# Neighbourhood attention taken in pairs of steps, with scores and transposes in one ring of four PSUM banks

## The chip, the cores and the metric

One core of one Trainium2 chip. The metric is the device time of one execution in microseconds; the kernel before is given by the median of three runs. Times of parts come from one profiled execution of it.

## The reference

One layer of an encoder, applied to two token groups, `x_prompt` (1024 tokens, 16 rows of 64) and `x_sample` (512 tokens, 8 rows): RMSNorm, two-dimensional neighbourhood attention with residual, RMSNorm, SwiGLU with residual, a final RMSNorm. Only the attention matters here. Width 1024, 16 heads of 64; a query at grid row r sees 8 rows of keys, and in them the 16 columns around its own, which are taken as bands of 32 columns for 16 query columns each:

```python
s = jnp.einsum('bjqhd,bkjchd->bhjqkc', qr, kr) * scale       # j: 4 column blocks, c: 32 key columns
s = jnp.where(valid_j, s + bias, -jnp.inf)
p = softmax(s over (k, c))                                    # 8 rows x 32 columns
o = jnp.einsum('bhjqkc,bkjchd->bjqhd', p, vr)
...
x = x + o @ w_o
x = x + swiglu(rms_norm(x, norm_ffn), w_gate, w_up, w_down)
```

All data is float32.

## The kernel before, in words

**Precision.** Every float32 operand of a large matmul is split into a high and a low half (`split`, lines 138 and 139 without scale: ScalarE (ACT) casts, VectorE (DVE) subtracts), and a product is made of three passes (`PASS`: high-high, high-low, low-high).

**Stages.** Norm of all tokens and V (0 to 180 us of the profile); attention (180 to 735 us); second norm and its operands; a feed-forward part with seven products in place of eight blocks (lines 708 to 819 and 837 to 937), which takes the rest. PSUM has eight banks of 128 x 512 float32. One pool holds four rings of two banks each: tag G for projections, S for scores, T for transposes, V for products. A ring's tile waits until the tile that had its bank before has been read.

**A step of attention.** The heads go in 8 pairs (hp), whose two heads lie on partitions 0 to 63 and 64 to 127. The prompt has per head pair two groups g of 512 queries, the sample one; per group there are four column blocks j. A step is one (hp, g, j): 64 steps in the prompt, 32 in the sample. `step` emits it in this order:

- `scores`, first half (line 394): three passes for two heads, six matmuls of 64 rows each into two S banks.
- `flip` of the step before (lines 420 to 424): each head's probabilities are transposed in 128 x 128 blocks (three in the prompt, two in the sample) into a T bank; ACT copies the high half to tile `pT` (423), DVE subtracts the low half (424).
- `scores`, second half: for each head DVE adds the bias and takes the maximum (402), ACT takes the exponential and the sum (405), DVE the reciprocal (407); head 0 is scaled by DVE (409), head 1 by ACT (411).
- Fillers: portions of six matmuls (lines 332 and 586) of other work, namely the next head pair's Q and K projections and, in the sample, the output projection. Four portions a projection; the last one also evacuates it (lines 342 to 350). Twelve matmuls a step in the prompt.
- `weighted` for the step before (431): products of V with pT into two V banks. Two steps (j = 0, 1 or 2, 3) share them, and after the second one `collect` adds the parts (441 ACT, 442 and 444 DVE) into `oT`, and GpSimd's queue stores it.

After a step come `fill_bias`, which allots and loads bias tiles ahead (lines 198 to 216; three ahead, ring of four; column blocks 1 and 2 share one), and `chores.do`: one weight or V block, loaded earlier by SyncE's queue (SP), is split by ACT and DVE (138 to 142), and the next is loaded. Two loads are under way at a time. V blocks are four DMAs each (line 378).

**Order.** The framework's planner takes the instructions in the program's order as priority and puts them into each engine's queue by its own estimates of when they are ready; each engine then runs its queue in order. So the queues follow the text above in the main, with exceptions where the planner found something not ready.

Of the kernel before, what the change touches and what calls it, by code (L numbers as in the profile page):

```python
# [55 lines left out]
def body(tc, xp, xs, g_mix, g_ffn, g_fin, w_qkv, rpb, w_o, w_g, w_u, w_d, yp, ys):  # L56
# [9 lines left out]
    with es:  # L66
# [39 lines left out]

        def psum(tag, name, bufs=None):
            return ps.tile([P, 512], F32, tag=tag, name=name, bufs=bufs)

# [14 lines left out]
        def transpose_split(xn, hh, hl, col):  # L124
            for b in range(2):
                pt = psum("T", "pt")
# [68 lines left out]
        q_cm, qpool = pool("qpool", bufs=2)  # L195
        b_cm, bpool = pool("bpool", bufs=4)

# [32 lines left out]
        def fill_bias():  # L230
            while len(ahead) < 3:
                n = next(bias_it, None)
# [182 lines left out]
        def flip(ss, n):  # L415
            out = []
            for s in ss:
                pt = psum("T", "ptt")
                for c in range(n):
                    nc.tensor.transpose(pt[:, c * P:(c + 1) * P], s[:, c * P:(c + 1) * P], ident)  # L420
                pT = ap.tile([P, 3, 2, P], F32R, tag="pT", name="pT", bufs=3)
                pv = pt[:, :n * P].rearrange("p (c q) -> p c q", q=P)
# [23 lines left out]

        def steps(hp, g, q, k, v, n, store):
            oT = ap.tile([P, 512], F32, tag="o", name="oT", bufs=2)
            ov = oT.rearrange("p (r j i) -> p j r i", r=8, j=NJ)
            b = None  # L450
            for jj in range(2):
                pos = []
                for u in range(2):
                    j = jj * 2 + u
                    if j != 2:
                        b = next_bias()
                    yield dict(
                        s=lambda b=b, j=j: scores(q, k, 4 * (g == 1), 4 * n, j, lambda h: b[:, h, :n * P]),
                        n=n, pos=pos, g=u, j=j, v=v,
                        dst=(lambda h, jj=jj: ov[h * HD:(h + 1) * HD, jj * 2:jj * 2 + 2]) if u else None,  # L460
                        done=(lambda: nc.gpsimd.dma_start(out=o_d[hp, :, g * 512:(g + 1) * 512], in_=oT))
                        if j == 3 else None)
                    fill_bias()

# [10 lines left out]

        def step(st, fillers, n):
            sc = st["s"]() if st else None
            if sc:
                next(sc)
            pT = None  # L480
            if prev:
                p, pss = prev.pop()
                pT = flip(pss, p["n"])
            ss = next(sc) if sc else None
            run(fillers, n)
            if pT:
# [50 lines left out]
        for hp in range(HP):  # L537
# [6 lines left out]
            if last:  # L544
# [14 lines left out]
        step(None, [], 0)  # L559
        k_cm.__exit__(None, None, None)  # L560

# [44 lines left out]
        for hp in range(HP):  # L606
# [13 lines left out]
        step(None, ofill, 2)  # L620
        a_cm.__exit__(None, None, None)
# [36 lines left out]
        def norm2(t):  # L658
# [5 lines left out]
            for b in range(2):  # L664
                pt = psum("T", "pt")
                for kk in range(4):
# [290 lines left out]
```

## Time and profile before

| what | us |
|---|---|
| median of 3 runs (lowest, highest) | 1846.19 (1841.29, 1848.37) |
| profiled execution | 1845.18 |
| its span | 1843.4 |
| PE busy in the span | 1754.1 |
| DVE, ACT, GpSimd busy | 1192.9, 863.7, 448.4 |
| attention, prompt (180 to 518.2) | 338.2 |
| attention, sample (518.2 to 735) | 216.8 |

The span is the profiled time from the first to the last instruction; 1.8 us of the execution lie outside it. PE is TensorE's matmuls, PEld its weight loads, which run beside them; SPq and POOLq are queues that issue DMAs. In a row of the timeline stand start, length, engine, line, operation, output tile <- input tiles, shape and count, and in brackets how long the engine had been idle before it and what ended that. Lengths of matmuls include their way through the array, so the next one starts before the last has ended; I reckon PE's time from start to start. In a row of groups stand busy time, mean ns of one, and idle time before.

### The profile page before, as it was taken

How to read it: one execution, taken by the hardware profiler on the slowest of the kernel's cores; microseconds unless marked ns; L12 is line 12 of the kernel's file. 1: busy time of each engine (PE TensorE's matmuls, PEld its weight loads, DVE VectorE, ACT ScalarE, POOL GpSimd, SP SyncE). 2: the span in 40 equal slices, each digit the busy share in tenths (PEclk: the TensorE clock that was granted, in tenths of full speed). 3: DMA queues.
4: the chain of work that ended last, by engine and by line, in shares of the span. 5: the costliest groups of instructions: out<-in, count | busy, mean ns of one | idle time of the engine just before them, and what ended most of it. 6: DMA issues, size and time to landing. Idle time of an engine off the chain costs nothing.

```text
span 1843.4 us, 25648 instructions
## 1 busy us (share of the span) xinstructions
PE 1754.1 (95%) x9178; PEld 1522.5 (83%) x9178; DVE 1192.9 (65%) x2191; ACT 863.7 (47%) x1706; POOL 448.4 (24%) x495
## 2 busy tenths in 40 slices
PE   8999999999999999979999999999999969999898
PEld 6877777777767777868999999899999958887676
DVE  4401877777896566768777777867777444545654
ACT  4411776766785554544443444444443333333322
POOL 1211000000130000112243342424243323526420
PEclk9999999999999999988999999999999979999999
DMA  7755334333464443676343434544333277635732
GB/s 245 221 183 160 111 105 113 108 101 103 126 208 146 133 149 100 221 247 185 108 121 118 133 110 151 164 129 125 108 120 107 68 272 245 225 130 191 232 129 100
DMA packets 222048, 278.80 MB, mean 151 GB/s; under 512 B 25600, under 2 KB 171776, under 8 KB 221920
## 3 DMA queue, kind: packets, MB, share of 16 engines
q1 hardware_dynamic: 201824, 210.69, 37.3%
q0 software_dynamic: 18368, 60.18, 9.5%
q10 hardware_dynamic: 1728, 6.29, 1.1%
q8 instruction: 72, 1.18, 0.3%
q14 instruction: 56, 0.46, 0.1%
HBM read 213.20 MB, written 76.43 MB: 157 GB/s over the span
## 4 chain that ended last, share of the span: by engine, by line
PE 68%; DVE 10%; DMA 9%; ACT 5%; issue 3%; SPq 2%; POOL 2%; DVEq 0%; ACTq 0%; POOLq 0%
PE pa L754 20%; PE pd L910 12%; PE pd L754 10%; PE pgv L278 7%; PE pg L332 6%; PE pb L754 5%; DMA vr<-v_d 5%; PE pgo L586 3%; DMA dr<-ffn_w_down 2%; PE pss L394 2%; PE ptt L420 2%; DVE pT L424 2%; SPq L378 2%; PE po L431 2%; ACT s L405 1%
## 5 line engine op out<-in xcount | busy, mean ns | idle before, releaser
L910 PE MATMUL pd<-wd,go 128*128 128x512 f32 x1386 | 323.0, 395 | 30.5 <-ACT go L138 20.4
L910 PEld LDWEIGHTS pd<-wd,go 128*128 128x128 f32 x1386 | 263.0, 191 | 90.4 <-ACT go L138 21.6
L754 PE MATMUL pa<-h,ws 128*128 128x384 f32 x1056 | 201.8, 339 | 2.9 <-ACT c L777 2.1
L754 PE MATMUL pa<-h,wa 128*128 128x384 f32 x1056 | 195.1, 338 | 7.0 <-ACT wa L138 4.5
L754 PE MATMUL pd<-h,ws 128*128 128x384 f32 x1056 | 198.3, 335 | 1.2 <-ACT h L138 0.6
L332 PE MATMUL pg<-hTp,whl 128*128 128x512 f32 x768 | 193.7, 399 | 0.0
L754 PEld LDWEIGHTS pa<-h,wa 128*128 128x128 f32 x1056 | 185.8, 190 | 8.9 <-ACT wa L138 5.2
L139 DVE TENSOR_TENSOR ws<-wt,ws 128x1024 fp32r<-128x1024 f32 x88 | 108.6, 1235 | 127.1 <-ACT ws L138 126.7
L754 PEld LDWEIGHTS pa<-h,ws 128*128 128x128 f32 x1056 | 185.1, 189 | 6.7 <-ACT c L777 4.3
L754 PEld LDWEIGHTS pd<-h,ws 128*128 128x128 f32 x1056 | 184.5, 188 | 1.8 <-ACT h L138 1.0
L332 PEld LDWEIGHTS pg<-hTp,whl 128*128 128x128 f32 x768 | 139.9, 188 | 27.5 <-issue 0.4
L805 POOL DMA_DIRECT2D gop_d<-c x66 | 50.5, 765 | 387.4 <-DVE c L796 380.3
L405 ACT ACTIVATE s<-s,mx 128x384 f32<-128x384 f32 (+1 forms) x192 | 110.7, 580 | 67.3 <-DVE mx L402 67.1
L586 PE MATMUL pgo<-wo,oh 128*128 128x512 f32 x576 | 139.3, 392 | 0.2 <-DVE oh L139 0.2
L139 DVE TENSOR_TENSOR wa<-wr,wa 128x512 fp32r<-128x512 f32 x132 | 117.8, 897 | 18.4 <-ACT wa L138 17.8
L138 ACT CAST ws<-wt 128x1024 fp32r<-128x1024 f32 x88 | 92.6, 1053 | 68.6 <-PE pd L754 65.4
L586 PEld LDWEIGHTS pgo<-wo,oh 128*128 128x128 f32 x576 | 105.6, 188 | 20.7 <-DVE oh L139 0.6
L138 ACT CAST go<-gr 128x1408 fp32r<-128x1408 f32 x42 | 57.7, 1374 | 131.2 <-PE pd L910 114.0
L138 ACT CAST wa<-wr 128x512 fp32r<-128x512 f32 x132 | 81.4, 621 | 62.8 <-PE pb L754 40.0
L754 PE MATMUL pb<-h,wa 128*128 128x384 f32 x528 | 102.0, 340 | 3.4 <-DVE c L774 3.4
L332 PE MATMUL pg<-hTs,whl 128*128 128x512 f32 x384 | 102.6, 404 | 0.8 <-DVE q L343 0.8
L424 DVE TENSOR_TENSOR pT<-ptt,pT 128x384 fp32r<-128x384 f32 (+1 forms) x192 | 90.0, 507 | 17.3 <-ACT pT L423 16.5
(138 smaller groups left out, 2859.6 us busy)
## 6 DMA issues: line engine op xcount, KB each, us to landing
gr<-gop_d SPq DMA_DIRECT2D x42, 704.0 KB
dr<-ffn_w_down SPq DMA_DIRECT2D x99, 256.0 KB
wr<-ffn_w_gate SPq DMA_DIRECT2D x44, 512.0 KB
wr<-ffn_w_up SPq DMA_DIRECT2D x44, 512.0 KB
wr<-na_w_qkv SPq DMA_DIRECT2D x38, 512.0 KB
gop_d<-gs POOLq DMA_DIRECT2D x88, 192.0 KB, 4.4
gop_d<-c POOLq DMA_DIRECT2D x66, 192.0 KB, 2.8
vr<-v_d SPq DMA_DIRECT2D x192, 64.0 KB
```

What stands on the lines that cost most here:

```text
L138: nc.scalar.copy(hi, raw)
L139: nc.vector.tensor_tensor(lo, raw, f32(hi), ALU.subtract)
L278: nc.tensor.matmul(pg, hh[a][:, k, c:c + P], wv[k // 2][b][:, k % 2], start=(k == 0 and i == 0), stop=(k == KB - 1 and i == 2))
L332: nc.tensor.matmul(pg, w[:, a, k, :], h[b][:, k, c:c + 512], start=(k == 0 and i == 0), stop=(k == KB - 1 and i == 2))
L378: nc.sync.dma_start(out=raw[:, j * P:(j + 1) * P], in_=src[:, BS[j]:BS[j] + 32, :])
L394: nc.tensor.matmul(pt[:, :n], q[h * HD:(h + 1) * HD, a, j].rearrange("p r i -> p (r i)"), kv[:, krow:krow + nrow, BS[j]:BS[j] + 32], start ...
L405: nc.scalar.activation(s[:, :n], s[:, :n], AF.Exp, bias=mx, scale=-1.0, accum_out=sm)
L424: nc.vector.tensor_tensor(pT[:, :n, 1], pv, f32(pT[:, :n, 0]), ALU.subtract)
L586: nc.tensor.matmul(pg, ohs[k // 4][:, a, k % 4], wo[:, b, k, n * 512:(n + 1) * 512], start=(k == 0 and i == 0), stop=(k == KB - 1 and i == 2))
L754: nc.tensor.matmul(bank[:, :HT], a(y, k), b[:, z, k], start=start and k == 0 and i == 0, stop=k == KB // 2 - 1 and i == 2, skip_group_chec ...
L805: nc.gpsimd.dma_start(out=gop_d[i, 3 * c:3 * c + 3, :, p].rearrange("j q t -> q j t"), in_=a.rearrange("q (j t) -> q j t", j=3))
L910: nc.tensor.matmul(pd, go[:, y, i], wds[i][:, z], start=(i == 0 and m == 0), stop=(i == NP - 1 and m == 2))
```

## The change

Two steps, column blocks 0 and 1 or 2 and 3, become one unit. Its twelve score matmuls of both blocks are emitted in one run into four banks of tag S. Then come the softmax of four heads, filler portions (`fill(0)`, two of them in the prompt), the products of the pair before with `collect`, and the two flips of this pair, each followed by one filler portion. The products are so one pair behind their scores, and the flips are in the pair itself. Tag T is gone: transposes take banks of tag S, which has four. Bias tiles are two ahead in a ring of three, `pT` has four buffers in place of three, and the chores of two steps come together after a pair. In the last head pair of the prompt a pair gets three filler portions (one per `fill`), where two steps had two. Transposes of the norms (lines 126 and 665) and one in four of the last products (906) use tag S in place of T.

```diff
         def psum(tag, name, bufs=None):
-            return ps.tile([P, 512], F32, tag=tag, name=name, bufs=bufs)
+            return ps.tile([P, 512], F32, tag=tag, name=name, bufs=4 if tag == "S" else 2)
...
-        b_cm, bpool = pool("bpool", bufs=4)
+        b_cm, bpool = pool("bpool", bufs=3)
...
         def fill_bias():
-            while len(ahead) < 3:
+            while len(ahead) < 2:
...
         def flip(ss, n):
...
-                pt = psum("T", "ptt")
+                pt = psum("S", "ptt")
...
-                pT = ap.tile([P, 3, 2, P], F32R, tag="pT", name="pT", bufs=3)
+                pT = ap.tile([P, 3, 2, P], F32R, tag="pT", name="pT", bufs=4)
...
         def steps(hp, g, q, k, v, n, store):
...
             for jj in range(2):
-                pos = []
-                for u in range(2):
-                    j = jj * 2 + u
+                sc = []
+                for j in (jj * 2, jj * 2 + 1):
                     if j != 2:
                         b = next_bias()
-                    yield dict(
-                        s=lambda b=b, j=j: scores(q, k, 4 * (g == 1), 4 * n, j, lambda h: b[:, h, :n * P]),
...
-                    fill_bias()
+                    sc.append(lambda b=b, j=j: scores(q, k, 4 * (g == 1), 4 * n, j, lambda h: b[:, h, :n * P]))
+                yield dict(s=sc, n=n, jj=jj, v=v, dst=...)
+                fill_bias()
...
-        def step(st, fillers, n):
-            sc = st["s"]() if st else None
-            if sc:
-                next(sc)
-            pT = None
-            if prev:
-                p, pss = prev.pop()
-                pT = flip(pss, p["n"])
-            ss = next(sc) if sc else None
-            run(fillers, n)
-            if pT:
-                if not p["g"]:
-                    p["pos"].extend((psum("V", "po"), psum("V", "po")))
-                weighted(pT, [x() for x in p["v"]], p["j"], p["n"], p["pos"], p["g"])
-                if p["dst"]:
-                    collect(p["pos"], p["dst"])
+        def step(st, fill):
+            sc = [x() for x in st["s"]] if st else []
+            for x in sc:
+                next(x)
+            ss = [next(x) for x in sc]
+            fill(0)
+            if prev:
+                p, pT = prev.pop()
+                pos = [psum("V", "po") for _ in range(2)]
+                for u in range(2):
+                    weighted(pT[u], [x() for x in p["v"]], p["jj"] * 2 + u, p["n"], pos, u)
+                collect(pos, p["dst"])
                 if p["done"]:
                     p["done"]()
+            pT = []
+            for u, x in enumerate(ss):
+                pT.append(flip(x, st["n"]))
+                fill(1 + u)
             if st:
-                prev.append((st, ss))
+                prev.append((st, pT))
...
+            def fill(part):
+                run(fillers, 1 if part or last else 2)
...
                 for st in steps(hp, g, (q0, q1)[g], k, vs[g:g + 3], 3, None):
-                    step(st, fillers, 1 if last else 2)
-                    if i in (0, 1, 2, 5, 6, 7) or last:
-                        chores.do()
-                    i += 1
+                    step(st, fill)
+                    for _ in range(2):
+                        if i in (0, 1, 2, 5, 6, 7) or last:
+                            chores.do()
+                        i += 1
...
+            def fill(part):
+                run(fillers, 1 if part else 2)
+                run(ofill, 1 if part else 2)
+
             for i, st in enumerate(steps(hp, 2, *qk, vs, 2, None)):
-                step(st, fillers, 2)
-                run(ofill, 2)
-                for _ in range((i + 1) * n // 4 - i * n // 4):
+                step(st, fill)
+                for _ in range((i + 1) * n // 2 - i * n // 2):
                     chores.do()
...
-                pd = psum("GSVT"[bank % 4], "pd")
+                pd = psum("GSVS"[bank % 4], "pd")
```

More of the change, by code (lines that the diff above doesn't have):

```diff
@@ L105, in in_order, with psum @@
                         mybir.DependencyClass.NoSync, mybir.DependencyReason.DATA), reason="in_order")
-        def psum(tag, name, bufs=None):
-            return ps.tile([P, 512], F32, tag=tag, name=name, bufs=bufs)
+        def psum(tag, name):
+            return ps.tile([P, 512], F32, tag=tag, name=name, bufs=4 if tag == "S" else 2)
         def bcast(ap):
@@ L125, in transpose_split @@
             for b in range(2):
-                pt = psum("T", "pt")
+                pt = psum("S", "pt")
                 for kk in range(4):
@@ L451, in steps @@
             for jj in range(2):
-                pos = []
-                for u in range(2):
-                    j = jj * 2 + u
+                sc = []
+                for j in (jj * 2, jj * 2 + 1):
                     if j != 2:
                         b = next_bias()
-                    yield dict(
-                        s=lambda b=b, j=j: scores(q, k, 4 * (g == 1), 4 * n, j, lambda h: b[:, h, :n * P]),
[L459 to L462, printed above, removed]
-                    fill_bias()
+                    sc.append(lambda b=b, j=j: scores(q, k, 4 * (g == 1), 4 * n, j, lambda h: b[:, h, :n * P]))
+                yield dict(s=sc, n=n, jj=jj, v=v, dst=lambda h, jj=jj: ov[h * HD:(h + 1) * HD, jj * 2:jj * 2 + 2],
+                           done=(lambda: nc.gpsimd.dma_start(out=o_d[hp, :, g * 512:(g + 1) * 512], in_=oT))
+                           if jj else None)
+                fill_bias()
         def run(fillers, n):
@@ L552, in body @@
                 for st in steps(hp, g, (q0, q1)[g], k, vs[g:g + 3], 3, None):
-                    step(st, fillers, 1 if last else 2)
-                    if i in (0, 1, 2, 5, 6, 7) or last:
-                        chores.do()
-                    i += 1
+                    step(st, fill)
[3 more added lines that the diff above has]
+                        i += 1
             drain(fillers)
             qk = nqk
-        step(None, [], 0)
+        step(None, lambda part: None)
         k_cm.__exit__(None, None, None)
@@ L619, in body @@
             qk = nqk
-        step(None, ofill, 2)
+        step(None, lambda part: run(ofill, 1))
         a_cm.__exit__(None, None, None)
@@ L664, in norm2 @@
             for b in range(2):
-                pt = psum("T", "pt")
+                pt = psum("S", "pt")
                 for kk in range(4):
```

## The prediction

> **What bounds the kernel now.** I read the page first, then a table by stage, then PE's timeline step by step.
>
> ```profile
> span 1843.4 us, 25648 instructions
> PE 1754.1 (95%) x9178; PEld 1522.5 (83%) x9178; DVE 1192.9 (65%) x2191; ACT 863.7 (47%) x1706; POOL 448.4 (24%) x495
> ```
>
> PE is busy 95% of the span, so a gain must come out of PE's idle time or make its work shorter. Only the attention changes. The table by stage (length, busy time of PE, PEld, DVE, ACT and POOL with instruction counts, granted clock, DMA share, GB/s), cut where the head pairs and the two request groups begin, has the prompt's first seven head pairs in rows 1 to 3, its last one in row 4, the sample in rows 5 to 7; the eighth row, of another cut, is the stage behind:
>
> ```profile
> 180.00:264.20 84.20, 81.10 (x468) 63.64 (x468) 66.23 (x191) 58.48 (x144) 5.87 (x15) 1.00 0.36 103
> 264.20:307.60 43.40, 42.00 (x242) 32.91 (x242) 34.51 (x99) 30.46 (x75) 3.09 (x8) 1.00 0.37 106
> 307.60:483.70 176.10, 167.92 (x962) 131.63 (x962) 138.14 (x393) 121.64 (x297) 12.38 (x32) 1.00 0.39 111
> 483.70:518.20 34.50, 33.47 (x189) 24.23 (x189) 30.67 (x90) 30.43 (x73) 6.57 (x6) 1.00 0.45 140
> 518.20:568.90 50.70, 46.50 (x256) 34.97 (x256) 45.66 (x123) 40.12 (x98) 17.15 (x8) 1.00 0.64 195
> 568.90:712.70 143.80, 138.69 (x723) 108.38 (x722) 85.34 (x256) 73.25 (x189) 7.60 (x14) 1.00 0.44 136
> 712.70:735.00 22.30, 22.30 (x130) 17.61 (x130) 16.48 (x54) 13.19 (x39) 2.17 (x4) 1.00 0.20 72
> ...
> 700.00:850.00 150.00, 136.01 (x664) 113.71 (x663) 100.47 (x198) 73.71 (x152) 17.55 (x30) 0.92 0.64 207
> ```
>
> Attention takes 555 us, and PE is bound there too. Rows 1 to 3 are 303.7 us for 7 x 4 pairs of steps, 10.85 a pair; DVE works (66.23 + 34.51 + 138.14) / 28 = 8.53 us of it, ACT 210.58 / 28 = 7.52. PE's timeline of one undisturbed step (start, length, instruction), with the score run cut open by narrower windows (its 2nd and 3rd couple of matmuls start at 302.61 and 302.79):
>
> ```profile
> 301.53 0.87 PE L431 MATMUL po<-pT,v 128*128 128x256 f32 x6
> 302.12 0.28 PE L431 MATMUL po<-pT,v 128*128 128x256 f32 x1
> 302.33 0.81 PE L394 MATMUL pss<-kp,q 64*128 64x384 f32 x6
> 302.61 0.52 PE L394 MATMUL pss<-kp,q 64*128 64x384 f32 x4
> 302.79 0.34 PE L394 MATMUL pss<-kp,q 64*128 64x384 f32 x2
> 303.06 0.87 PE L420 MATMUL ptt<-ident,s 128*128 128x128 f32 x6
> 303.69 3.01 PE L332 MATMUL pg<-hTp,whl 128*128 128x512 f32 x12
> 306.54 0.87 PE L431 MATMUL po<-pT,v 128*128 128x256 f32 x6
> 307.58 0.44 PE L394 MATMUL pss<-kp,q 64*128 64x384 f32 x2 [0.17 <-ACT kp L349]
> ```
>
> Start to start: scores 0.73, transposes 0.63, twelve projection matmuls 2.85, products 0.80: 5.01 a step, 10.02 a pair. So 10.85 - 10.02 = 0.83 a pair, 23.1 us over 28 pairs, is stall. The last row shows one kind: at a new head pair the scores wait for the evacuation of K. The others, ACT, DVE and PE together:
>
> ```profile
> 278.30 0.62 ACT L138 CAST v<-vr 128x512 fp32r<-128x512 f32 x1 [1.91 <-DMA vr<-v_d]
> 279.33 1.02 DVE L424 TENSOR_TENSOR pT<-ptt,pT 128x384 fp32r<-128x384 f32 x2 [2.06 <-ACT pT L423]
> 279.94 1.09 PE L431 MATMUL po<-pT,v 128*128 128x256 f32 x6 [0.41 <-DVE pT L424]
> ...
> 287.49 0.52 PE L420 MATMUL ptt<-ident,s 128*128 128x128 f32 x3 [0.21 <-DVE ri L407]
> 288.34 0.55 PE L420 MATMUL ptt<-ident,s 128*128 128x128 f32 x3 [0.33 <-ACT s L411]
> ```
>
> ACT stands in its queue before a V split whose load has not landed; the copies of pT behind it are late, DVE's subtractions behind those, and the products wait. Eight microseconds on, transposes wait for the softmax. In the sample, three starts of score runs:
>
> ```profile
> 599.44 0.63 PE L394 MATMUL pss<-ks,q 64*128 64x256 f32 x6
> 607.38 0.63 PE L394 MATMUL pss<-ks,q 64*128 64x256 f32 x6
> 614.50 0.38 PE L394 MATMUL pss<-ks,q 64*128 64x256 f32 x1
> ```
>
> A clean step is 614.50 - 607.38 = 7.12, the one before it took 7.94. The stretch of 143.8 us has 19 steps, from its 114 score matmuls, six a step:
>
> ```profile
> L394 PE MATMUL pss<-ks,q 64*128 64x256 f32 x114 | 11.9, 315 | 0.0
> ```
>
> So 143.8 - 19 x 7.12 = 8.5 us are stalls there.
>
> **The change, part by part.** *One score run instead of two.* A score run costs more than its couples' pace of 0.18 (302.61 to 302.79): entry is 0.21 after the last product where products follow each other at (302.12 - 301.53) / 5 = 0.12, the first couple takes 0.28, and from the last couple to the transposes 0.27. That is 0.09 + 0.10 + 0.09 = 0.28 us a run, in a change between 64-row and 128-row matmuls. One run less a pair saves 0.28; 32 prompt and 16 sample pairs give 13.4 us. The bounds: nothing, if the planner cuts the run up again, and these 13.4, since the three surpluses are all that the rows show.
>
> *Products one pair behind.* Now pT is used 2.85 us after its transposes, one projection block. Then the second flip is followed by 6 projection matmuls (1.4), 12 scores (1.27) and 12 projection matmuls (2.85): 5.5 us. The ACT wait of 1.91 then fits inside. I count waits of the products at nothing; the cover is the twelve matmuls of fill(0), and where it lacks (the last pair of the prompt, whose 8 filler portions are spent 3, 3, 2, 0) up to 2 us show once.
>
> *Softmax of four heads, then two flips.* From the groups of one head pair (busy, mean ns):
>
> ```profile
> L405 ACT ACTIVATE s<-s,mx 128x384 f32<-128x384 f32 x16 | 9.8, 614 | 6.3 <-DVE mx L402 6.2
> L402 DVE CUSTOM_DVE_ANT_0 s<-pss,bp 128x384 f32<-128x384 f32 x16 | 8.4, 549 | 0.1
> L424 DVE TENSOR_TENSOR pT<-ptt,pT 128x384 fp32r<-128x384 f32 x16 | 8.2, 551 | 2.1 <-ACT pT L423 2.1
> L423 ACT CAST pT<-ptt 128x384 fp32r<-128x384 f32 x16 | 6.9, 479 | 1.4 <-PE ptt L420 1.4
> L411 ACT ACTIVATE s<-s,ri 128x384 f32<-128x384 f32 x9 | 5.5, 616 | 1.6 <-DVE ri L407 1.6
> L442 DVE TENSOR_TENSOR tmp<-tmp,po 64x256 f32<-64x256 f32 x8 | 3.4, 419 | 3.6 <-ACT tmp L441 3.5
> L139 DVE TENSOR_TENSOR v<-vr,v 128x512 fp32r<-128x512 f32 x4 | 2.8, 689 | 0.0
> L350 DVE TENSOR_TENSOR kp<-pg,kp 128x512 fp32r<-128x512 f32 x3 | 2.1, 692 | 0.9 <-ACT kp L349 0.9
> L139 DVE TENSOR_TENSOR whl<-wr,whl 128x1024 fp32r<-128x1024 f32 x1 | 1.2, 1224 | 0.8 <-ACT whl L138 0.8
> ```
>
> Count from the start of the score run. PE reaches the first flip at 1.27 + 2.85 + 12 x 0.12 = 5.55, the second after six transposes and six projection matmuls, 0.63 + 1.43 later, at 7.6. From the first reduction, the first two heads need about 0.55 + two exponentials 1.23 + reciprocal and scaling, about 0.8, with hand-overs 2.8 us; the other two 2 x 0.61 + 0.62 more, 4.7. So DVE may begin as late as 2.8 (5.55 - 2.8; 7.6 - 4.7 = 2.9). The scores are there at 0.8; ahead of them in DVE's queue stand the last subtractions of pT (to about 0.2), a Q or K subtraction 0.69 and the weight chores, now done back to back behind the pair: a V split 0.69, or V and a Q or K weight 1.91. That is 1.6 in pairs with one chore, 2.8 in pairs with two: no slack left in those. I take 0.5 us of stall in the 14 two-chore pairs and 0.15 in the other 14: 9 us, with ends at 0 and 14 x 1.2 (a whole weight subtraction shown).
>
> *Four banks in one ring.* Scores now wait for the banks of the flips before them. The second flip at 7.6 has its last subtraction 0.3 (three transposes) + 0.48 + 2 x 0.55 later, at 9.5, with hand-overs 9.9; the scores that take these banks start at 9.74 + 0.5. Slack about 0.5 us, so nothing in the plain case. DVE gets there in time only because the four additions of the products (4 x 0.42) lie ahead of the flips; they start at 5.55 and are done by 7.3.
>
> *The boundary of head pairs.* The last portion of K's projection now stands directly before the next head pair's scores; the products that hid it (0.80) are gone. Today's 0.17 becomes 0.17 + 0.80 = 0.97, and the second pass reads the low half, 0.69 of DVE later, part of it under the first couples: 1.3, seven times, 9 us. Ends: 0.17 (PE is given other matmuls meanwhile) and 1.7.
>
> *Biases, SP, POOL.* Three bias buffers with two ahead: the tile for the second step is loaded once the step before has been reduced, about 8 us ahead of its use, against two issues of about 0.6 us on SP; POOL's fills move with it. V loads are issued in twos at a pair's end and used at the next one's; their number is the same. I cost these at nothing: the cover is a whole pair, 9.74 us, and if a load lands late it costs what today's V splits show, 1.91 on ACT.
>
> **The sum.** Prompt, seven head pairs: stalls 23.1 now, 9 + 9 = 18 after, gain 5. Sample: of 8.5 us of stall I take half away, 4 us, since the waits of products go but ACT still meets late loads. Row 4 and row 5: the dense chores stay; the bare last pair costs about 1.5. In all 13.4 + 5 + 4 - 1.5 = 21 us. The profiled execution took 1845.2 us (span 1843.4 and 1.8 around it), 1.0 below the median of 1846.2. 1845.2 - 21 = 1824.2, on the median's scale 1825.
>
> **The rivals.** *The ring closes a loop (slower).* Place: the release of a flip's bank. V splits still stand in ACT's queue; if one waits just ahead of the second flip's copies, subtraction, bank, next scores and the whole of PE shift by it, where today scores and transposes own two banks each. It decides from a stall of 10.85 - 9.74 = 1.1 us a pair. Every prompt pair has a V split, and the waits of 180 to 520 us show
>
> ```profile
> ACT v L138 <- DMA vr<-v_d: 20.5, 12, 2.8
> ```
>
> that is 1.7 us each. At 1.7 in each of 28 pairs, and nothing gained in the sample: 28 x 0.6 = 17 more, 1863. For it: DVE has 8.53 of 9.74 us to do; against it: slack 0.5 at that point, and loads issued a pair ahead.
>
> *The run is cut up.* The planner already split a run (307.58 is a run of two scores, then transposes). If it does so in each pair, the 13.4 us are not gained: 1838.
>
> *The ring never waits.* Stalls are left at the boundaries alone, seven times 1.0, and the sample's go: 13.4 + 16 + 8.5 = 38 gained, 1808.
>
> *The clock.* All seven rows of attention show a clock of 1.00, though PE idled 555.0 - 532.0 = 23 us there in short pieces; the stage behind shows 0.92. If waits on banks took attention to 0.92, 532 us of PE work would grow by 46: 1871. The Trainium skill, "TensorE: Matmul & The Clock Gate", section "A second HAM failure mode: psum-queue depth-cycling", says that a kernel cycling through PSUM banks can pause PE often enough between groups to swing its clock. By that rule the change, with its one ring, would end at the last time named; by this trace, which has such pauses at full clock, it does not.
>
> **How the numbers follow.** Forecast 0.50, ring without waits 0.14, run cut up 0.18, closed loop 0.15, clock 0.03. 0.5% is 9 us, about what a measurement of this kernel can tell from no change, so the borders are 1837 and 1855. Faster: the forecast but for its upper tail, 0.46, 0.14, and the lower end of the cut-up case, 0.05: 0.65. Slower: the loop, the clock, less the loop's mild end: 0.16. The rest 0.19. The range reaches from just below the ring without waits, 1806, to 1850, between the cut-up run and the loop; 0.07 lie below, 0.13 above. The forecast's own range is 1812 to 1838.
>
> **What would show it.** Right: the score run comes as twelve matmuls, starts of head pairs lie 40 to 42 us apart (43.4 now), products wait for nothing, couples inside the run keep 0.18. Wrong: PE rows of scores with idle time ended by DVE's pT subtraction (the loop), score runs of two, four or six (cut up), transposes ended by ACT's scaling for over 0.5 us in most pairs. The stages outside attention should keep their lengths within 3 us; a gain there would have another cause. What would most easily make the forecast wrong is the order in which ACT and DVE get chores and copies, which no row of before shows.

## The result, and the profile after

| | median us | runs |
|---|---|---|
| before | 1846.19 | 7, 1841.29 to 1852.67 |
| changed | 1838.88 | 7, 1832.59 to 1841.12 |

The ratio is 0.9949, interval 0.9926 to 0.9972: 0.5% faster, by the medians 7.3 us, where 21 us were forecast. The time lies in the range; the sign was right, the size a third. Page of the changed kernel, its span and its engines:

```profile
span 1830.8 us, 25624 instructions
PE 1745.4 (95%) x9178; PEld 1529.2 (84%) x9178; DVE 1190.4 (65%) x2191; ACT 858.2 (47%) x1706; POOL 449.2 (25%) x495
```

This execution (1832.59 us) was the shortest of the seven. The same kernel once more, for a second profile, had a median of 1834.2 us (4 runs, ratio 0.9929, interval 0.9907 to 0.9951) and a profiled span of 1837.1. Tables by stage, cut at the second head pair, the last one, the sample, the last product of attention and the end of the feed-forward (length, busy PE, PEld, DVE, ACT, POOL, granted clock, DMA share, GB/s), first the changed kernel:

```profile
220.90:480.30 259.40, 249.18 (x1441) 199.03 (x1440) 205.09 (x589) 180.91 (x445) 19.51 (x48) 0.99 0.40 111
480.30:517.90 37.60, 35.46 (x204) 27.78 (x203) 34.35 (x96) 31.59 (x76) 7.43 (x8) 1.00 0.45 134
517.90:728.20 210.30, 200.49 (x1076) 160.75 (x1076) 142.93 (x422) 119.30 (x317) 26.40 (x26) 0.98 0.47 145
728.20:1470.90 742.70, 726.29 (x4076) 709.00 (x4075) 536.59 (x723) 321.47 (x535) 238.37 (x259) 0.99 0.45 139
1470.90:1830.80 359.90, 322.82 (x1389) 263.14 (x1387) 189.87 (x204) 120.03 (x173) 123.38 (x89) 0.95 0.57 195
```

and the kernel before at the same points:

```profile
220.20:483.70 263.50, 251.88 (x1442) 197.46 (x1442) 207.13 (x589) 182.51 (x445) 18.57 (x48) 1.00 0.38 110
483.70:518.20 34.50, 33.47 (x189) 24.23 (x189) 30.67 (x90) 30.43 (x73) 6.57 (x6) 1.00 0.45 140
518.20:733.90 215.70, 206.38 (x1099) 160.03 (x1100) 146.91 (x430) 125.82 (x323) 26.91 (x26) 1.00 0.46 144
733.90:1481.30 747.40, 728.97 (x4071) 708.90 (x4069) 537.08 (x723) 321.44 (x535) 238.25 (x259) 0.98 0.45 138
```

Six head pairs gained 4.1 us together (43.9 to 43.2 each), the first and the last one lost 0.4 and 3.1, the sample gained 5.4: attention 6 us in all. The rest of the 12.6 us between these two spans lies behind attention (4.7 up to the end of the feed-forward, 2.2 in the 362 us of the last products, which took 364 in the second profile). Only the first 6 us are the change's stage.

PE's timeline over two pairs of the changed kernel (start, length, instruction, and what ended the idle time before):

```profile
318.22 1.86 PE L394 MATMUL pss<-kp,q 64*128 64x384 f32 x12
320.02 3.01 PE L332 MATMUL pg<-hTp,whl 128*128 128x512 f32 x12
322.87 1.60 PE L431 MATMUL po<-pT,v 128*128 128x256 f32 x12
324.30 0.82 PE L420 MATMUL ptt<-ident,s 128*128 128x128 f32 x6
324.87 1.64 PE L332 MATMUL pg<-hTp,whl 128*128 128x512 f32 x6
326.35 1.08 PE L420 MATMUL ptt<-ident,s 128*128 128x128 f32 x6
327.18 1.63 PE L332 MATMUL pg<-hTp,whl 128*128 128x512 f32 x6
329.66 2.20 PE L394 MATMUL pss<-kp,q 64*128 64x384 f32 x12 [0.85 <-DVE pT L424]
331.79 3.02 PE L332 MATMUL pg<-hTp,whl 128*128 128x512 f32 x12
```

The score run is one run of twelve, and the products (322.87) wait for nothing. But the score run takes 1.80 and 2.13 us start to start instead of 1.27, and between 327.18 and 329.66 six projection matmuls and a wait take 2.48 instead of 1.57. What ACT and DVE did there:

```profile
325.68 0.62 ACT L138 CAST v<-vr 128x512 fp32r<-128x512 f32 x1 [1.73 <-DMA vr<-v_d]
327.25 0.87 DVE L442 TENSOR_TENSOR tmp<-tmp,po 64x256 f32<-64x256 f32 x2 [0.22 <-ACT tmp L441]
327.63 1.63 ACT L423 CAST pT<-ptt 128x384 fp32r<-128x384 f32 x4
328.15 0.87 DVE L444 TENSOR_TENSOR oT<-tmp,po 64x256 f32<-64x256 f32 x2
329.05 1.95 DVE L424 TENSOR_TENSOR pT<-ptt,pT 128x384 fp32r<-128x384 f32 x4
...
339.55 0.68 DVE L139 TENSOR_TENSOR v<-vr,v 128x512 fp32r<-128x512 f32 x1
340.14 1.01 DVE L424 TENSOR_TENSOR pT<-ptt,pT 128x384 fp32r<-128x384 f32 x2
```

At 325.68 ACT meets a V block that has not landed, as before the change; now the copies of both flips are behind it, all four together at 327.63, and DVE's four subtractions, which free the banks, run from 329.05 to 331.0, into the next score run. Ahead of them on DVE stand the four additions of the products (327.25 to 329.0). They too are late through ACT, whose copy (441) is behind the V split; the forecast had them done 7.3 us after the start of the scores, here it is 10.8. At 339.55 the planner has put a V subtraction between the first and the second flip's, and the scores from 340.27 wait again. The waits of the changed kernel from 180 to 480 us (total, times, longest):

```profile
PEld pss L394 <- DVE pT L424: 18.8, 42, 1.3
PE pss L394 <- DVE pT L424: 5.3, 7, 0.9
ACT v L138 <- DMA vr<-v_d: 15.8, 10, 2.6
```

The first row is idle time of the weight loads of score matmuls, the second that of the matmuls themselves; neither is PE's loss as it stands, which has to be read from start to start. The head pair from 308.77 to 351.33 us took 42.56; four clean pairs of 9.74 would be 38.96. Its 3.6 us of stall are four score runs (0.18, 0.53, 0.86, 0.40 over 1.27), the wait of 0.91 behind 327.18, and 0.26 and 0.46 in front of transposes. The first of these score runs is the head pair's boundary; the other three and the 0.91, together 2.7 us, are waits for the banks.

### The profile page after: what moved, and what is told of

Same layout as the page of the kernel before. It is cut to its first block, busy times and chain, and to the rows that moved or that the text cites. A ratio compares the mean times of both kernels' runs of the same rounds, so it can differ in the third digit from the quotient of the medians.

```text
span 1830.8 us, 25624 instructions
## 1 busy us (share of the span) xinstructions
PE 1745.4 (95%) x9178; PEld 1529.2 (84%) x9178; DVE 1190.4 (65%) x2191; ACT 858.2 (47%) x1706; POOL 449.2 (25%) x495
## 4 chain that ended last, share of the span: by engine, by line
PE 69%; DMA 12%; DVE 7%; ACT 4%; issue 3%; SPq 2%; POOL 2%; DVEq 0%; ACTq 0%; POOLq 0%
PE pa L762 19%; PE pd L918 12%; PE pd L762 10%; PE pg L332 7%; PE pgv L278 7%; DMA vr<-v_d 5%; PE pb L762 5%; PE pgo L590 4%; DMA dr<-ffn_w_down 3%; PE pss L394 3%; SPq L378 2%; PE po L431 2%; PE ptt L420 1%; DMA gr<-gop_d 1%; DMA wr<-o_d 1%
## 5 line engine op out<-in xcount | busy, mean ns | idle before, releaser
L332 PE MATMUL pg<-hTp,whl 128*128 128x512 f32 x768 | 200.1, 405 | 0.0
L332 PE MATMUL pg<-hTs,whl 128*128 128x512 f32 x384 | 107.0, 415 | 1.9 <-DVE q L343 1.9
L139 DVE TENSOR_TENSOR go<-gr,go 128x1408 fp32r<-128x1408 f32 x42 | 73.9, 1760 | 43.6 <-ACT go L138 34.0
```

Source lines behind the costliest of these rows:

```text
L139: nc.vector.tensor_tensor(lo, raw, f32(hi), ALU.subtract)
L332: nc.tensor.matmul(pg, w[:, a, k, :], h[b][:, k, c:c + 512], start=(k == 0 and i == 0), stop=(k == KB - 1 and i == 2))
```

## The experiments

All are variants of the changed kernel where nothing else is said. Ratios are to the kernel before, run beside each. "A head pair" is the mean distance of the prompt's second to last head pair.

**The ring: score run in two, or the last portion later.** Two edits give the second flip's banks 1.4 us more:

```diff
-            for x in sc:                                   # e1
+            for u, x in enumerate(sc):
                 next(x)
+                fill(u)                                    # one portion behind each half of the scores
...
-            fill(0)
...
-                fill(1 + u)
+                fill(2 + u)
...
-                run(fillers, 1 if part or last else 2)
+                run(fillers, 0 if last and part > 1 else 1)
...
-                run(fillers, 1 if part or last else 2)     # e4: 1, 1, 2 in place of 2, 1, 1
+                run(fillers, 2 if part == 2 and not last else 1)
```

The sample's `fill` is changed in the same way in both.

> The changed kernel with its score run cut in two: scores of the first block, one filler portion, scores of the second block, one portion, then products, flip, portion, flip, portion. It leaves nothing out. In the changed kernel's trace a score run of twelve takes 1.45 to 2.2 us instead of 1.27, 1.9 us too long per head pair, with PE waiting for DVE's subtraction of pT. Theory 1 (the ring of four banks is the loss): the second block's banks get 1.4 us more time, so about 1.2 of the 1.9 us per head pair go, against 4 x 0.28 for the extra change between 64 and 128 rows: about even, 1835 to 1841 us. Theory 2 (the softmax of four heads is late, the ring only shows it): the second block's softmax has 1.4 us less cover, the second flips wait 0.5 to 1 us in each pair: 1850 to 1870. Theory 3 (the longer run saves nothing, my 0.28 was wrong): 1827 to 1832.

> The changed kernel with one filler portion moved from ahead of the products to behind the second flip (1, 1, 2 instead of 2, 1, 1 in prompt and sample). Nothing left out. Theory 1 (ring): the banks of the second flip get 1.4 us more before the next scores, score runs go to 1.3 to 1.5 us, which gives back 1.5 us per head pair and more; the first flip's softmax has 1.4 us less cover, so that some of it returns as waits of transposes; 1828 to 1836. Theory 2 (softmax late): transposes wait 1 us and more in each pair, 1850 to 1880.

Measured: e1 1838.1 us (10 runs, 0.9961, interval 0.9949 to 0.9972), a head pair 43.30; e4 1835.1 (4 runs, 0.9942, 0.9921 to 0.9963), 41.62. A score run and its successor of e4, then its waits and stages (six head pairs, sample):

```profile
323.65 1.33 PE L394 MATMUL pss<-kp,q 64*128 64x384 f32 x12
324.91 1.65 PE L332 MATMUL pg<-hTp,whl 128*128 128x512 f32 x6
...
PEld ptt L420 <- ACT s L411: 16.6, 30, 0.9
PEld pss L394 <- DVE pT L424: 2.8, 8, 0.4
...
220.50:470.20 249.70, 242.99 (x1441) 193.89 (x1440) 204.91 (x589) 180.33 (x445) 19.50 (x48) 1.00 0.42 116
507.80:729.20 221.40, 203.79 (x1076) 162.50 (x1076) 144.00 (x422) 119.41 (x317) 26.48 (x26) 0.96 0.44 138
```

A run of twelve without waits takes 1.26 us (forecast 1.27). With room for the banks, the scores' wait goes from 18.8 to 2.8 us, part of it turns up before the transposes, and a head pair gets 1.6 us shorter. The ring was the loss in the prompt; theory 2, softmax late, is out as its main cause. In the sample the same edit cost 11 us, so the total hardly moved; about 5 of the 11 are clock, which stood at half there for 17 us against 7 in the changed kernel. e1 came out even, as theory 1 said; by its account, what the cut gives the ring, the second change of rows takes back.

**DVE's queue: V's subtraction to GpSimd.**

```diff
-            split(rv, vv[:, :, 0:4:3, :], vv[:, :, 1:3, :])
+            nc.scalar.copy(vv[:, :, 0:4:3, :], rv)
+            nc.gpsimd.tensor_tensor(vv[:, :, 1:3, :], rv, f32(vv[:, :, 0:4:3, :]), ALU.subtract)
```

> The changed kernel with the low half of every V split subtracted by GpSimd instead of DVE (48 of 0.69 us). Nothing left out. Theory 1 (ring of banks, held up by DVE's queue, where V's subtraction stands between the two flips' subtractions): score runs get shorter by 0.3 us in most pairs, head pairs of the prompt 42.0 to 42.5 us apart instead of 43.2; 1828 to 1833 us. Theory 2 (late V loads, which stop ACT's queue, are what makes the banks late; DVE has room): no change, 1836 to 1841.

1835.6 us (4 runs, 0.9949, 0.9932 to 0.9965): by the total neither theory's figure. A head pair fell to 41.1, further than theory 1 said, but the first one took 41.8 (40.8 without) and the sample 218.7 us, 8 more, with its clock at half for 17 us against 7. ACT's waits for V loads fell too, from 14.4 to 6.0 us between 220 and 480, so the edit does not tell DVE's load and the late loads apart. Both cures together, GpSimd in the prompt alone:

> The changed kernel with the prompt's filler portions as 1, 1, 2 and the low half of the prompt's V blocks subtracted by GpSimd; the sample as in the changed kernel. Nothing left out. Theory 1 (the prompt's loss is the ring of banks, held up by DVE's queue; the two cures take it from two sides): head pairs 40.0 to 41.0 us apart (43.2 changed, 41.6 and 41.1 with one cure each), the sample 210 to 214 us; 1826 to 1832. Theory 2 (each cure takes away one and the same burst of waits, the late V load once a head pair): 41 us as with one cure, 1830 to 1835.

1827.3 us (4 runs, 0.9904, 0.9885 to 0.9923), a head pair 41.2, the sample 207.1. By the head pair the two do not add: they cure the same waits, theory 2. The total lies in theory 1's range and not in theory 2's. The sample, left alone, was 3 us shorter than in the changed kernel, and attention had no half clock in this execution, where the changed kernel's had 10.2 us; the first head pair took 43.4, 2.6 more.

**The last head pair.**

```diff
-    run(fillers, 1 if part or last else 2)
+    run(fillers, (0 if last else 2) if part == 0 else 1)
```

> The changed kernel, but in the prompt's last head pair a pair of steps gets two filler portions (after the first and after the second flip, none ahead of the products) instead of three, so that the eight portions last for all four pairs. Nothing left out. In the changed kernel this head pair takes 37.6 us, before the change 34.5. Theory 1 (the last pair bare of fillers is the loss): 35.5 or less, total 2 us less than the changed kernel, 1836. Theory 2 (the dense weight chores of this head pair are the loss, whatever the portions): 37 to 39, total unchanged.

The last head pair took 37.2 us (37.6 without): theory 2. Median 1838.6 (10 runs, 0.9961, 0.9946 to 0.9975). The bare pair that I had priced is 0.5 of these 3 us at most; what costs the rest was not found. This execution showed something else. Stages and PE at one place of it, and, last, two rows of the changed kernel's own profile after the same burst of waits (the score run at 329.66):

```profile
284.00:287.70 3.70, 2.81 (x16) 1.61 (x14) 3.60 (x9) 2.67 (x6) 0.00 (x0) 1.00 0.39 112
287.70:291.20 3.50, 3.50 (x10) 2.76 (x10) 3.42 (x13) 3.01 (x9) 0.30 (x1) 0.55 0.45 115
...
287.75 4.61 PE L332 MATMUL pg<-hTp,whl 128*128 128x512 f32 x12
292.20 1.58 PE L431 MATMUL po<-pT,v 128*128 128x256 f32 x12
...
328.04:331.74 3.70, 2.81 (x16) 1.59 (x14) 3.61 (x9) 2.65 (x6) 0.00 (x0) 1.00 0.31 84
331.74:335.24 3.50, 3.50 (x18) 2.95 (x18) 3.43 (x13) 3.01 (x9) 0.30 (x1) 1.00 0.55 134
```

After the burst of waits the clock went to half for 3.4 us (0.55 in the mean of the row), and twelve projection matmuls took 4.45 us instead of 2.85, with no wait. In the changed kernel the same burst left the clock at 1.00.

**The planner's order.** Here an edge is added from the last copy (ACT) and subtraction (DVE) of the pair's flips to the instructions of the chores that follow the pair in the program, so that the planner cannot put those ahead in the queues (lines are 9 further down):

```diff
                 pT.append(flip(x, st["n"]))
+                for e in (nc.scalar, nc.vector):
+                    behind[e.engine] = <last instruction so far on e>
...
                     work(r)                    # in Chores.do
+                    for i in <instructions that work(r) gave>:
+                        if i.engine in behind:
+                            tc.add_manual_dep(i, behind[i.engine].name, <order only>)
```

> The changed kernel with the order of ACT's and DVE's queues bound at one place: the splits of V and of weights may not be put ahead of the last flip's copies and subtractions of the pair before them in the program, where the planner has put many of them earlier. Nothing left out. Theory A (the planner puts V splits so early that ACT meets loads that have not landed, and the flips' copies behind them are late): ACT's waits for V loads in 220 to 480 us go from 14 us to under 4, the long score runs and the slow second flip vanish, head pairs 41.5 to 42.3 us apart, 1828 to 1834. Theory B (DVE has simply too much to do between flip and scores): the splits now delay the reductions instead, transposes wait, 43 to 45 us a head pair, 1838 to 1846.

1825.9 us (4 runs, 0.9902, 0.9883 to 0.9922). A head pair of 41.15, and in the waits from 180 to 480 us no row of ACT waiting for a V load is left. Stages (six head pairs, the last one), and the starts of a pair's score run and of what follows the pair:

```profile
220.60:467.50 246.90, 244.54 (x1443) 197.50 (x1442) 205.97 (x589) 179.98 (x444) 19.49 (x48) 1.00 0.42 116
467.50:507.10 39.60, 35.66 (x187) 27.21 (x186) 33.54 (x96) 29.11 (x73) 7.22 (x7) 0.86 0.46 139
...
332.72 1.34 PE L403 MATMUL pss<-kp,q 64*128 64x384 f32 x12
342.40 0.40 PE L440 MATMUL po<-pT,v 128*128 128x256 f32 x2
```

A clean pair is 9.68 us long, 0.06 under my 9.74. Theory A holds: it was where the planner put the splits, not DVE's load, that made the banks late; nothing but the order was changed. Whether ACT's stop before a V load or DVE's V subtraction between the flips weighs more is not parted, since the edge moves both. It cures half of the stall: 41.15 is still 2.2 us over four clean pairs. Scores still wait for banks, in

```profile
PEld pss L403 <- DVE pT L433: 8.4, 24, 0.7
```

and of the four score runs of the head pair that ends at 344.02, two still take 1.51 and 1.72 us. The run cut in two, with this order:

> The kernel with the bound order of chores, with its score run cut in two as in the kernel with two runs. Nothing left out. With the late V loads and the ring out of the way, this prices the longer run by itself. Theory A (one run less is worth 0.28 us a pair): head pairs 42.0 to 42.5 us apart against 41.15, total 1834 to 1842 against 1826. Theory B (the room of 1.4 us that the cut gives the ring is worth as much, as it was without the bound order): 41.0 to 41.6, total 1824 to 1830.

1835.6 us (6 runs, 0.9947, 0.9929 to 0.9965), a head pair 41.64: at the edge of B's range for the head pair, in A's for the total. So the longer run is worth 0.5 us a head pair here, not the 1.1 of its price. One of four runs, 0.28 us, is cut anyhow in the bound order, at the head pair's boundary (four scores, a projection matmul, eight scores); the rest may be the room that the cut gives the ring, which this run does not part from it.

**What of this is the change's own.** The same edge in the kernel before, everywhere and in the prompt's first seven head pairs alone, and the latter in the changed kernel:

> The kernel before with the same bound order: chores are not put ahead of the flip of the step that they follow in the program. No part of the change. Theory A (early V splits cost the kernel before its 1.2 to 1.9 us a head pair too, but the rest is the change's own): head pairs 42.0 to 43.0 us apart against 43.9, total 1833 to 1841. Theory B (the bound order is worth to the kernel before as much as to the changed one, 2.1 us a head pair; the change itself brings under 1 us): 41.8 or less, total under 1833. Theory C (chores then stand ahead of the reductions, and nothing is gained): 43.5 to 44.5, 1842 to 1850.

> The changed kernel with the bound order in the prompt's first seven head pairs alone; the last one and the sample are left to the planner. Nothing left out. In the kernel with the bound order everywhere the last head pair took 39.6 us (37.6 without) and the sample's first two 49.5 (41.4 without), with the clock at half for 24 us. Theory A (the dense chores of that stretch want the planner's order): last 37 to 38, sample 207 to 212, total 1814 to 1821. Theory B (that loss was the clock of one execution): total 1824 to 1828.

> The kernel before with the bound order of chores in the prompt's first seven head pairs alone, as the fastest kernel so far (1819) has it on top of the change. No part of the change. Theory A (with the order right, the change is worth what its trace shows: 0.4 us a head pair and some 5 us of the sample): 1824 to 1830. Theory B (the change brings nothing of its own): 1816 to 1822. Head pairs 41.5 us apart in both; the sample 214 to 217 in A, 207 to 210 in B.

| | order bound | median us | ratio (interval) | a head pair | sample |
|---|---|---|---|---|---|
| before, e10 | everywhere | 1825.9 (4 runs) | 0.9894 (0.9865 to 0.9924) | 41.55 | 212.2 |
| changed, e6 | everywhere | 1825.9 (4 runs) | 0.9902 (0.9883 to 0.9922) | 41.15 | 214.3 |
| before, e13 | seven | 1839.3 (5 runs) | 0.9956 (0.9939 to 0.9973) | 41.55 | 217.0 |
| changed, e11 | seven | 1819.0 (4 runs) | 0.9852 (0.9833 to 0.9872) | 41.12 | 207.1 |

The rows behind it, e11 first, then e13 (six head pairs, the last, the sample):

```profile
219.80:466.50 246.70, 244.27 (x1443) 197.41 (x1442) 205.90 (x589) 180.23 (x445) 19.52 (x48) 1.00 0.41 116
466.50:506.30 39.80, 36.21 (x200) 27.77 (x199) 34.07 (x97) 31.99 (x76) 7.46 (x8) 0.96 0.50 152
506.30:713.40 207.10, 198.34 (x1075) 159.37 (x1075) 143.22 (x422) 119.53 (x317) 26.35 (x26) 0.99 0.48 148
```

```profile
219.40:468.80 249.40, 245.16 (x1443) 197.11 (x1442) 208.96 (x589) 183.30 (x445) 18.52 (x48) 1.00 0.40 113
468.80:509.10 40.30, 38.62 (x191) 26.93 (x190) 30.73 (x88) 29.30 (x69) 6.55 (x6) 0.96 0.49 145
509.10:726.10 217.00, 208.57 (x1098) 160.95 (x1098) 147.29 (x432) 126.87 (x327) 27.09 (x26) 1.00 0.46 144
```

In the prompt's head pairs the order alone gives the kernel before 2.4 us (43.9 to 41.55), and the change gives 0.4 more. In the sample the change is worth 9.9 us in the pair of e11 and e13, nothing in the pair of e10 and e6. So the total of what the change brings, with the order bound, came out at 0 in one setting and about 20 us in the other. Part of the zero is clock: from the last head pair on, attention in e6 had it at half for 24 us, in e10 for 10, which is some 7 us. The 20 are not clock (7 us at half in e11, 3 in e13); what in the order around the change makes them was not found. e10 came out as its theory B said (under 1833). e13 met neither theory: its total lies above both ranges, its sample at the upper end of A's. e11 is the fastest kernel of the study, 27 us under the kernel before by the medians of this table and the first, 26 beside its own runs. GpSimd on top of it:

> The same, and the low half of the prompt's V blocks subtracted by GpSimd. Nothing left out. Theory 1 (DVE's 8.5 us a pair is what is left of the loss): head pairs 40.0 to 40.6 us apart against 41.15, total 5 us below the one without it, 1810 to 1816. Theory 2 (what is left is the head pair's boundary and switches, which GpSimd does not touch): 41 us, the same total.

1828.0 us (4 runs, 0.9902, 0.9883 to 0.9921), a head pair 41.46: slower, which neither theory had; 4 of the 9 us are there when the second head pair starts. GpSimd's subtraction helped here only where the planner's own order stood.

**Products behind, alone.** The kernel before, its products one step further behind, with four `pT` buffers and, as in the changed kernel, bias tiles two ahead in three buffers:

```diff
-            pT = None
+            flipped = None
...
-                pT = flip(pss, p["n"])
+                flipped = p, flip(pss, p["n"])
...
-            if pT:
+            if late:
+                p, pT = late.pop()
...
+            if flipped:
+                late.append(flipped)
```

> The kernel before with one part of the change alone: products one step further behind their transposes, with single steps, separate rings for scores and transposes, portions and chores as before, four pT buffers and three bias buffers. Nothing left out. Theory 1 (own rings let the later products take away the wait that follows a late V load, and no new wait appears; the ring of four costs the changed kernel what its longer run gains): head pairs of the prompt 42.2 to 42.8 us apart (43.9 before), 1832 to 1838. Theory 2 (the stall only moves to the next place in ACT's queue, to transposes and scores): 43.5 to 44 us, 1843 to 1848.

1854.0 us (4 runs, 1.0049, 1.0030 to 1.0068), slower. PE and ACT at the V split of one head pair, and the one head pair of the six that kept full clock:

```profile
328.34 0.71 PE L332 MATMUL pg<-hTp,whl 128*128 128x512 f32 x2
331.17 0.55 PE L420 MATMUL ptt<-ident,s 128*128 128x128 f32 x3 [2.12 <-ACT s L411]
331.48 4.12 PE L332 MATMUL pg<-hTp,whl 128*128 128x512 f32 x10
...
329.98 0.62 ACT L138 CAST v<-vr 128x512 fp32r<-128x512 f32 x1 [2.33 <-issue]
...
402.23:446.01 43.78, 40.97 (x241) 32.80 (x240) 34.37 (x99) 31.08 (x75) 2.92 (x8) 1.00 0.38 103
```

The products' wait goes, and ACT's stop at a V split now holds up the scaling of the softmax and with it the transposes, for 2.12 us. (This row names no releaser for the stop; the five others from 220 to 480 us, 11.6 us in all, ended with the load.) So theory 2, and what is worse than it goes with the clock: the other five head pairs had it at half for 3.4 or 6.8 us, as behind 331.48, and took 44.9 to 46.3; the one without took 43.8, about what the kernel before takes (43.9). V blocks also live a step longer here, in the same five buffers; how much of the stop is that was not parted.

**Side effect in the feed-forward.**

```diff
-            pa, pb, pd = psum("G", "pa"), psum("V", "pb"), psum("S", "pd")
+            pa, pb, pd = psum("G", "pa"), psum("V", "pb"), psum("ST"[bankturn[0] % 2], "pd")
```

> The kernel before, with one thing alone of the change's side effects: the feed-forward's accumulator pd alternates between tags S and T, so that it has four banks as in the changed kernel, instead of two. Attention as before. From the last product of attention to the end of the feed-forward the profile of before shows 747 us, those with the change 743 to 744. Theory 1 (the four banks give these 3 to 4 us): 743 to 744, total 1842. Theory 2 (that is run-to-run and half-clock time): 746 to 748, total 1846.

1843.9 us (10 runs, 0.9999, 0.9988 to 1.0009), 746.8 us from the last product to the feed-forward's end: no effect. All profiles of the changed kernel and its variants show 742.7 to 744.9 there, those of the kernel before, e7, e10 and e13 746.8 to 748.7, but e8 742.6. What these 3 to 4 us are stays open; e8 shares with the changed kernel the later products and the numbers of bias and `pT` buffers.

**The spread.**

> The changed kernel once more, unaltered, for a second profile. Its times ran from 1832.6 to 1841.1 and the profiled execution was among the shortest. Theory A (the spread is TensorE's clock, which falls to half for 3.4 us after a burst of waits, or not, by where its window lies): this profile has more than the first one's 10.2 us of half clock in attention where it is longer, about 0.5 us of span for each further microsecond. Theory B (the spread is loads landing late): as much half clock as before, and longer waits of ACT for V.

The second profile is 6.3 us longer in span. Its clock stood at half for 72.5 us in all against 65.8, 13.7 against 10.2 in attention (none in the kernel before's), which by the expectation's half explains 3.3; ACT's waits for V loads in attention are the same (51.0 and 50.6). The last products took 4.2 more. So theory A accounts for half of these two. The eleven executions on record go the same way: the three at a mean clock of 0.981 or 0.982 took 1838.9 to 1841.1 us, the three at 0.985 or 0.986 1833.1 to 1833.6.

## Why the prediction was right or wrong

- *One score run instead of two, 13.4 us:* the price per run was right (1.26 for a clean run; a clean pair 9.68 against 9.74). It was not gained where the planner cuts runs at boundaries, and cutting every run again cost only 0.1 us a head pair in e1 and 0.5 in e9 against the priced 1.1.
- *Products one pair behind:* right, their waits are gone. It is not worth anything by itself (e8): the stop of ACT that caused them stayed, and meets the next in its queue.
- *Softmax of four heads, 9 us or 1.3 a head pair:* too much. In the head pair worked out above transposes waited 0.26 and 0.46, the latter in the pair at the boundary.
- *Four banks in one ring, "nothing in the plain case":* this is the step that failed. The slack (called 0.5; its own figures, 9.9 and 10.24, give 0.3) was worked out for queues in the program's order. The planner had put V subtractions between the flips' subtractions and V splits ahead of their loads, so that the scores' weight loads waited for banks 42 times, 18.8 us in 180 to 480 us; in the head pair worked out above that is 2.7 us of PE. Stall was 43.24 - 38.96 = 4.3 us a head pair where the forecast had 18 / 7 = 2.6. In the first seven head pairs it came to 300.2 - 28 x 9.74 = 27.5 us instead of 18, so that the gain of 5 us became a loss. These 9.5 us are most of the 15 by which attention missed the forecast. With the order bound (e6) the stall was 2.2 a head pair, under the forecast's.
- *V loads "cost at nothing":* the second half of the same error. I had the row of 1.91 us and let it vanish behind the products' cover, but ACT's copies and with them the banks had none. It is the mechanism of the slower rival, which was to decide from a stall of 1.1 us a pair: measured were 4.3 / 4 = 1.07, of which 0.5 went with the order bound. That the change still came out ahead in the prompt is the longer run's doing (28 x 0.28 = 7.8 us against 4.2 more of stall).
- *Boundary, 1.3 us a head pair:* too much. The planner moved four projection matmuls ahead, and 0.18 in the scores and 0.46 before transposes were left.
- *Last head pair:* forecast about even, it lost 3.1, and e3 shows that the portions were 0.5 of it at most; the rest stays open. The sample, forecast at 8.5 with its share of the runs, gave 5.4 and, in the second profile, 6.8.
- *The clock, chance 0.03:* too low as a mechanism, though far from the 0.92 priced. Attention's clock fell to 0.98 and 0.99, and 10 to 14 us at half cost some 5 to 7. Over all executions, the mean clock was 0.9857 for the kernel before (49 executions beside the experiments) and 0.9834 for the changed one (11); the difference is some 4 of 1840 us. By the rule of the Trainium skill, "TensorE: Matmul & The Clock Gate", section "A second HAM failure mode: psum-queue depth-cycling", pauses between groups can swing the clock; the rows at 284 to 291 us of e3 agree. The changed kernel's rows at 328 to 335 us show the same pauses without the swing.

The forecast's 1825 was reached by the same kernel with the order of the chores bound (1825.9), and the kernel before reaches it so as well. That e6 meets the total is in part luck: its first seven head pairs ended 16 us earlier than before the change where 13 were forecast, its last one lost 5 where about none was, and its sample gained 1.4 where 8.5 was.

## What to carry to other kernels

Where a planner fills the queues, work out slack in the order that the queues have and not in the program's, and take every wait for a load that the trace of before shows as one that stays on its engine until something moves it: making one reader of that engine later (e8) only passed the wait to the next. Before restructuring, bind the order of such side work and look again: here one edge brought more than the change. A ring that two stages share ties the second's start to the slowest engine that frees the first's banks. And read the granted clock of each stage before a difference of half a per cent is put down to an edit: in e8, e4 and e6 it was a large part of what seemed to be the edit's.

## What the runs showed that I had not expected

Waits need not be long to cost clock: in the 3.7 us ahead of the half clock in e3 PE was busy for 2.81, and the next twelve matmuls took 1.6 us more. But such waits do not always cost it. The code of the first seven head pairs is the same in three profiles, and so is the burst of waits once a head pair. From the second to the seventh head pair the changed kernel's first profile had one stretch at half clock, the second three, and e3 five. Stretches at half in attention lasted 3.41 us or a multiple of it. Those five began at 288.08, 332.45, 376.83, 421.20 and 465.57, that is 44.37 us apart, thirteen times 3.41, with head pairs 44.15 us long on average. So it seems to matter where a burst falls in a fixed rhythm of 3.41 us; no run shifted a burst on purpose to show it. In the kernel before, with the same amount of waiting in other places (PE idle for 23 of 555 us), attention had no half clock at all.
